# VectorE's low halves issued one step later, and one step order for both halves of the output projection

## The chip, the cores and the metric

The kernel runs on one core of a Trainium2 chip. The metric is the device time of one execution in microseconds. Before the change the median of three runs is 1422.09 us (1421.06 to 1422.41). The core has five engines that run side by side, each with its own queue in order: TensorE (PE: matrix products, and PEld, the loading of its stationary operand), VectorE (DVE), ScalarE (ACT), GpSimd (POOL) and SyncE (SP, which issues the loads here). An instruction waits on semaphores until what it needs is there, and everything behind it on its engine waits with it.

## The reference

One transformer-like encoder layer on 256 tokens of width 2048, all in float32: three attention mixers, gated and merged, an output projection with a residual, then a gated feed-forward block with a residual. What matters here:

```python
h = rms_norm(x, g_mix)
proj = h @ w_in                                   # q, k, v of three mixers, and three gates
...
mkv = rms_norm(mem, g_mem) @ w_mem_kv             # keys and values of the memory tokens
...
gates = sigmoid(gt).reshape(b, s, 3, 2048)
merged = (gates[:, :, 0] * (oa @ w_br_a) + gates[:, :, 1] * (ob @ w_br_b)
          + gates[:, :, 2] * (oc @ w_br_c))
x = x + merged @ w_o
hf = rms_norm(x, g_ffn) @ w_ffn_in                # 2 x 5632 wide
x = x + (silu(hf[..., :5632]) * hf[..., 5632:]) @ w_ffn_out
```

## The kernel before

**Precision.** TensorE takes a rounded float32 type (fp32r). Each operand is split into a high half (`whi`, ScalarE copies the value into the rounded type) and a low half (`wlo`, VectorE subtracts the high half from the value). A product is three matmuls: high by high, high by low, low by high. So every weight block of 128 x 1024 values that SP loads (tile `raw`, six buffers) needs one ScalarE copy (line 364), then one VectorE subtraction (line 365), and the high and low tiles have four buffers each, with one more in a pool of its own for every fifth block behind the merging.

**Passes.** `pair` (line 369) computes two adjoining column blocks of 512 for all 256 tokens, over a string of steps such as `STEPS_O`. Two consecutive blocks of the contraction form a pair u. A step `d` or `D` does a pair in the plain way for the first or the second column block: one load, four products, twelve matmuls. A pair can instead be done for both column blocks at once with seven products in place of eight, in the steps f, g and h and a share in p and q. These use sums of weight blocks and sums of token blocks (`forms`). On VectorE, step g begins with three adds of 128 x 512 (lines 455 to 457), step h with one (line 471), p and q with none; f, g, p and q then have one block to split and h half a block. Steps f and g issue six matmuls each, h three, p and q up to six.

The products go into six PSUM banks X, Y, Z, W, V, Q. X, Y and Z come from a pool of four banks (tag "at") and W, V and Q from another four (tag "mm"). The transposes take banks from both pools too. Behind the steps, ScalarE copies X and W out, VectorE subtracts (lines 489 and 492) and adds the banks (lines 413 and 414), and a function given by the stage takes the result.

**Order.** `run` (line 511) goes through the steps of all passes. For each step `ready()` issues the loads, the sums, the high half and the low half; the step's products are issued four steps later (three in the memory projection). The framework's planner orders each engine's instructions by its own estimates, but TensorE and SP keep program order, and `nc.follow` (line 364 on) chains the high halves on ScalarE, and the sums and low halves on VectorE, in the order of the program. Work that is not chained, such as evacuations and residual adds, the planner sets between them. Side work (transposes, squares, token sums) runs as generators that `tick` moves on by one piece behind each step's products.

**Stages.** The memory projection (`w_mem`) is a `pair` of plain steps. The projections into q, k and v and the first gates use `product`, which splits in another place (lines 125 and 126). Then `run(everything(), 4)` does the merging (four gate passes, each followed by a branch pass), the output projection in two halves (n = 0 and n = 2), and the feed-forward block: eleven passes into the hidden layer (0 to 10), with two passes of `w_ffn_out` behind passes 3, 7 and 10. Behind each w_o half VectorE adds the residual (line 785), ScalarE squares (line 791), TensorE transposes the new x block by block, and ScalarE and VectorE split the transposed block out of PSUM into `x1T` (lines 128 and 129), which the hidden passes read. Behind the first w_o half the token sums of `x1T` are formed too (lines 712 to 714 and 723).

Of the kernel before, what the change touches and what calls it, by code (L numbers as in the profile page):

```python
# [11 lines left out]
F32 = mybir.dt.float32  # L12
# [41 lines left out]
STEPS_GATE = "d0 D0 d4 D4 f1 d5 g1 D5 h1 f2 g2 d6 h2 f3 g3 h3 p0 p2 D6 q0 q2 d7 D7".split()  # L54
STEPS_FFN = "d0 D0 d1 D1 d4 D4 f2 d5 g2 D5 h2 f3 d6 g3 h3 p0 D6 q0 d7 D7".split()
STEPS_O = "d0 D0 d1 D1 f2 d4 g2 D4 h2 d5 f3 D5 g3 d6 h3 p0 D6 q0 d7 D7".split()
STEPS_O2 = "d0 f2 D0 g2 d1 h2 f3 D1 g3 d4 h3 p0 D4 q0 d5 D5 d6 D6 d7 D7".split()
STEPS_OUT = "d0 D0 d1 D1 d2 D2 f6 d3 g6 D3 h6 f7 d4 g7 h7 p0 D4 q0 d5 D5".split()
STEPS_OUT2 = "d0 f5 D0 g5 d1 h5 f6 D1 g6 d2 h6 f7 D2 g7 d3 h7 p0 p2 D3 q0 q2 d4 D4".split()

# [39 lines left out]
def encoder_block(ctx: ExitStack, tc: tile.TileContext, a: dict, out: bass.AP):  # L100
    nc = InOrder(tc)
# [10 lines left out]
    def s8(shape, name, dt=F32R, pool=None):  # L112
        return (pool or big).tile(shape, dt, name=name, tag="s8")

    def s4(shape, name, dt=F32):
        return mid.tile(shape, dt, name=name, tag="s4")
# [35 lines left out]
    def row_scale(ss, r):  # L152

        v = small.tile([P, T], F32, name="rs_v")
        nc.vector.tensor_scalar(v, ss, 1.0 / D, EPS, op0=ALU.mult, op1=ALU.add)
        y = rsqrt(v, [P, T], nc.vector)
        nc.vector.tensor_copy(r[:, 0], y)
        nc.vector.tensor_mul(r[:, 1], y, y)
# [4 lines left out]
    def advance(job):  # L163

        try:
            lag = next(job[1])
            job[0] = now[0] + (lag or 1)
            return lag is not None
        except StopIteration:
            side.remove(job)  # L170
            return True

    def start(steps):

        job = [0, steps]
        side.append(job)
        advance(job)

    def tick():
        now[0] += 1  # L180
        for job in list(side):
            if job[0] <= now[0] and advance(job):
                break

    def urgent(steps):

        while True:
            with tc.high_priority():
                try:
                    lag = next(steps)  # L190
                except StopIteration:
                    return
            yield lag
# [74 lines left out]
    def transposed(src, dst, g=None, lag=1, also=None):  # L268


        for h in range(2):
            if h:
                yield lag
            tp = bank("tp", "mm" if h and nc.on else "at")
            for k in range(2):
                for t in range(T):
                    nc.tensor.transpose(tp[:, k * S + t * P:k * S + (t + 1) * P],
                                        src[t][:, (2 * h + k) * P:(2 * h + k + 1) * P], ident)
            if g is None:
                d = dst(2 * h, 2)  # L280
                split(d[0], d[1], tp.rearrange("p (k s) -> p k s", s=S))
                if also:
                    full = s4([P, 4, P], "ffull")
                    nc.scalar.activation(full, tp.rearrange("p (b s) -> p b s", s=P), AF.Copy)
                    also(h, full)
            else:
                for k in range(2):
                    d = dst(2 * h + k, 1)
                    split(d[0], d[1], tp[:, k * S:(k + 1) * S], g(2 * h + k))
# [64 lines left out]
    def halves(*srcs):  # L354

        count[0] += 1
        pool, n = (more[0], 1) if more and count[0] % 5 == 0 else (wp, 4)
        hi = pool.tile([P, PK, NC], F32R, name="whi", bufs=n)
        lo = pool.tile([P, PK, NC], F32R, name="wlo", bufs=n)
        n = 0  # L360
        for v in srcs:
            v = v.unsqueeze(1) if len(v.shape) == 2 else v
            o = slice(n, n + v.shape[1])
            nc.follow(nc.scalar.activation(hi[:, o], v, AF.Copy))  # L364
            nc.follow(nc.vector.tensor_sub(lo[:, o], v, hi[:, o].bitcast(F32)))  # L365
            n += v.shape[1]
        return hi, lo

    def pair(src, lhs, order, done, forms=None, operand=None):

# [46 lines left out]
        def whole(u, c):  # L417
            def ready():
                if operand and c == 0:
                    operand(2 * u, True)  # L420
                raw = load((src(u, c),), 0, PK)
                if operand and c == 0:
                    if 2 * u + 2 < KT:
                        operand(2 * u + 2, True)
                    operand(2 * u)
                hi, lo = halves(raw)

                def products():
                    for k in range(2):
                        for t in range(T):  # L430
                            mul(("YV", "ZQ")[c][t], at(2 * u + k, t), hi[:, k], lo[:, k])
                return products
            return ready
# [76 lines left out]

    def run(pairs, ahead):

        nc.on = True
        waiting = []
        for p in pairs:
            for products in p:
                waiting.append(products)
                if len(waiting) > ahead:
                    waiting.pop(0)()
                    tick()  # L520
        for products in waiting:
            products()
            tick()
        nc.on = False

    whole_k = lambda n: [d + str(u) for u in range(n) for d in "dD"]
    block_pair = lambda w, n: lambda u, c: w[n + c][u]
# [146 lines left out]
    def beginning():  # L674
# [4 lines left out]
                   lambda c, r: start(take_slots(r, MEM_SLOTS[4 * c:4 * c + 4], r_m, "mem", nc.vector)), operand=memT)  # L679

    run(beginning(), 3)
    oT = [s8([P, 4, 2, S], f"oT{i}") for i in range(3)]
    ol = lambda k: (oT[k // 4][:, k % 4, 0], oT[k // 4][:, k % 4, 1])
# [33 lines left out]
    def sums_of(lhs, these, room):  # L717

        def steps():
            for u, to in zip(these, room):  # L720
                full = s4([P, 4, P], "ffull")
                for k in range(2):
                    nc.vector.tensor_add(full[:, 2 * k:2 * k + 2].rearrange("p t s -> p (t s)"),
                                         *(v.bitcast(F32) for v in lhs(2 * u + k)))
                token_sums(full, to)
                yield 1
        start(steps())
        return by_pair(these, room)
# [4 lines left out]
    def form_room(n, pool=None):  # L733
        tiles = [s8([P, 2, 2, 4, P], "forms", pool=pool) for _ in range((n + 1) // 2)]
        return [tiles[i // 2][:, i % 2] for i in range(2 * len(tiles))]
# [38 lines left out]
    def projecting():  # L774
        x.extend(s8([P, D], f"x{t}", F32) for t in range(T))
        for t in range(T):
            nc.sync.dma_start(out=x[t], in_=a["x"][t * P:(t + 1) * P, :])
        x1T.extend(s8([P, 2, 4, S], "x1T") for _ in range(4))
        mTl = lambda k: (mT[k // 4][:, 0, k % 4], mT[k // 4][:, 1, k % 4])
        oforms = sums_of(mTl, (2, 3), form_room(2))  # L780
        for n in (0, 2):
            def add(c, r, n=n):
                xc = [x[t][:, (n + c) * NC:(n + c + 1) * NC] for t in range(T)]
                for t in range(T):
                    nc.vector.tensor_add(xc[t], r[:, t], xc[t])

                def later():
                    yield 1
                    sq = s4([P, T, NC], "sq")
                    for t in range(T):  # L790
                        nc.scalar.activation(sq[:, t], xc[t], AF.Square, accum_out=ss1[:, t, n + c:n + c + 1])
                    yield 2
                    yield from transposed(xc, lambda k, m: (x1T[n + c][:, 0, k], x1T[n + c][:, 1, k]),
                                          lambda k: gT[:, 2, 4 * (n + c) + k:4 * (n + c) + k + 1], 2)
                    if n + c == 1:
                        room.extend(form_room(3))
                        forms.append(sums_of(x1l, (1, 2, 3), room[:3]))
                    elif n + c == 3:
                        yield 2
                        ssr = small.tile([P, T], F32, name="ss", bufs=1)  # L800
                        nc.vector.tensor_reduce(ssr, ss1, axis=AX.X, op=ALU.add)
                        row_scale(ssr, r_f)
                start(urgent(later()))
            yield pair(block_pair(a["w_o"], n), mTl, STEPS_O2 if n else STEPS_O, add, oforms)


    def store(t, o):
# [53 lines left out]
    def everything():  # L861
        for stage in (merging, projecting, feeding):
            yield from stage()

    run(everything(), 4)
    finish()

# [83 lines left out]
```

## Time and profile before

| what | value |
|---|---|
| median of three runs | 1422.09 us |
| the profiled execution | 1422.27 us, its span 1420.3 us |
| granted clock of TensorE, mean | 0.995 |
| TensorE busy | 1393.0 us, 98% of the span, 6248 matmuls |
| VectorE busy | 1118.9 us, 79%, 1474 instructions |
| ScalarE busy | 796.6 us, 56%, 1093 instructions |
| traffic | 277.08 MB, 195 GB/s on average |

In the profile a line names the kernel's line, the engine, the operation, the tile written and the tiles read, then the shapes. A matmul's duration overlaps with that of the next, so the distance between starts tells the pace. L75 is the line of the helper that issues all of TensorE's and SP's instructions, so TensorE's work is told apart by bank (mmX, mmY and so on) and operand. "Idle before" is time in which the engine stood still ahead of an instruction, with the instruction that ended it.

### The profile page before, as it was taken

The numbers are of one execution on the slowest core, as the hardware profiler recorded it, in microseconds if no ns is written. First come the engines' busy times: TensorE is split into PE (matmuls) and PEld (weight loads), VectorE is DVE, ScalarE is ACT, GpSimd is POOL, SyncE is SP. The second block draws the span as 40 slices with busy tenths as digits, with TensorE's granted clock in tenths as the row PEclk, the third lists the DMA queues.
The fourth block names the chain that finished last, engine by engine and source line by source line (L and its number), as shares of the span: only waits on it lengthen the run. The fifth ranks groups of instructions, "written<-read, shape, count | busy, mean of one in ns | idle before, by whom it ended". The sixth has DMA issues, their size and how long they took to land.

```text
span 1420.3 us, 17529 instructions
## 1 busy us (share of the span) xinstructions
PE 1393.0 (98%) x6248; PEld 1138.2 (80%) x6248; DVE 1118.9 (79%) x1474; ACT 796.6 (56%) x1093; POOL 76.5 (5%) x146
## 2 busy tenths in 40 slices
PE   8999999999999999997999999999999999999998
PEld 6778878888878888886888888888888888888887
DVE  6767756754788888877888888988888988988863
ACT  6756545644464564654665556554566654465642
POOL 0025532200000000000000000000000000000000
PEclk9999999999999999998999999999999999999999
DMA  8976445456565675754655557565556656555653
GB/s 297 340 237 210 152 134 174 156 168 193 183 207 178 189 229 162 281 163 133 203 178 183 192 181 236 178 194 200 189 188 207 203 184 205 193 193 195 218 174 125
DMA packets 79415, 277.08 MB, mean 195 GB/s; under 512 B 8992, under 2 KB 11552, under 8 KB 79072
## 3 DMA queue, kind: packets, MB, share of 16 engines
q1 hardware_dynamic: 79184, 275.94, 59.7%
q8 instruction: 49, 0.80, 0.2%
q14 instruction: 38, 0.31, 0.1%
q10 hardware_dynamic: 144, 0.02, 0.0%
HBM read 273.05 MB, written 2.88 MB: 194 GB/s over the span
## 4 chain that ended last, share of the span: by engine, by line
PE 79%; DVE 8%; ACT 4%; issue 4%; POOL 2%; DMA 2%; SPq 0%; ACTq 0%; DVEq 0%; POOLq 0%
PE mm L75 15%; PE mmV L75 13%; PE mmY L75 13%; PE mmZ L75 13%; PE mmQ L75 11%; PE mmX L75 8%; DVE wlo L365 3%; ACT whi L364 3%; PE mmW L75 2%; DMA raw<-in_w_mem 1%; PE tp L75 1%; DVE raw L456 1%; DVE wlo L126 1%; POOL rot L584 1%; PE sc L75 1%
## 5 line engine op out<-in xcount | busy, mean ns | idle before, releaser
L365 DVE TENSOR_TENSOR wlo<-raw,whi 128x1024 fp32r<-128x1024 f32 (+1 forms) x454 | 515.7, 1154 | 155.3 <-ACT whi L364 153.3
L364 ACT ACTIVATE whi<-raw 128x1024 fp32r<-128x1024 f32 (+1 forms) x454 | 443.1, 1000 | 339.8 <-DVE raw L471 102.1
L75 PE MATMUL mm<-whi,xT 128*128 128x512 f32 x768 | 244.1, 394 | 0.0
L126 DVE TENSOR_TENSOR wlo<-raw,whi 128x1024 fp32r<-128x1024 f32 x100 | 128.7, 1296 | 86.0 <-ACT whi L125 85.5
L75 PEld LDWEIGHTS mm<-whi,xT 128*128 128x128 f32 x768 | 144.0, 189 | 29.6 <-issue 0.8
L125 ACT ACTIVATE whi<-raw 128x1024 fp32r<-128x1024 f32 x100 | 105.6, 1070 | 89.3 <-PE mm L75 81.5
L75 PE MATMUL mm<-wlo,xT 128*128 128x512 f32 x384 | 151.0, 393 | 0.1
L75 PE MATMUL mmY<-whi,x1T 128*128 128x512 f32 x288 | 112.5, 392 | 0.0
L75 PE MATMUL mmV<-whi,x1T 128*128 128x512 f32 x288 | 109.7, 393 | 0.0
L75 PE MATMUL mmZ<-whi,x1T 128*128 128x512 f32 x224 | 87.5, 391 | 0.0
L75 PE MATMUL mmQ<-whi,x1T 128*128 128x512 f32 x224 | 87.4, 390 | 0.0
L75 PEld LDWEIGHTS mm<-wlo,xT 128*128 128x128 f32 x384 | 72.6, 189 | 15.7 <-issue 0.8
L75 PE MATMUL mmX<-whi,forms 128*128 128x512 f32 x232 | 78.9, 392 | 0.0
L365 DVE TENSOR_TENSOR wlo<-t,whi 128x1024 fp32r<-128x1024 f32 x74 | 70.7, 990 | 4.6 <-ACT whi L364 4.6
L75 PEld LDWEIGHTS mmY<-whi,x1T 128*128 128x128 f32 x288 | 54.0, 188 | 12.0
L75 PEld LDWEIGHTS mmV<-whi,x1T 128*128 128x128 f32 x288 | 54.0, 188 | 11.7
L75 PE MATMUL mmY<-whi,hT 128*128 128x512 f32 x156 | 60.6, 393 | 0.0
L364 ACT ACTIVATE whi<-t 128x1024 fp32r<-128x1024 f32 x74 | 60.6, 859 | 0.0
L75 PE MATMUL mmV<-whi,hT 128*128 128x512 f32 x156 | 60.2, 392 | 0.0
L75 PE MATMUL mmY<-wlo,x1T 128*128 128x512 f32 x144 | 56.3, 391 | 0.0
L75 PE MATMUL mmV<-wlo,x1T 128*128 128x512 f32 x144 | 56.3, 391 | 0.0
L75 PE MATMUL mmZ<-whi,hT 128*128 128x512 f32 x136 | 53.9, 396 | 0.0
(258 smaller groups left out, 2706.6 us busy)
## 6 DMA issues: line engine op xcount, KB each, us to landing
raw<-in_w_ffn SPq DMA_DIRECT2D x176, 512.0 KB, 4.1
raw<-in_w_gate SPq DMA_DIRECT2D x96, 512.0 KB, 4.2
raw<-in_w_ffn_out SPq DMA_DIRECT2D x88, 512.0 KB, 4.3
raw<-in_w_qkv SPq DMA_DIRECT2D x64, 512.0 KB, 4.5
raw<-in_w_o SPq DMA_DIRECT2D x32, 512.0 KB, 4.2
raw<-in_w_br SPq DMA_DIRECT2D x24, 512.0 KB, 3.6
raw<-in_w_mem SPq DMA_DIRECT2D x16, 512.0 KB, 6.2
rawT<-in_memT SPq DMA_DIRECT2D x8, 256.0 KB, 4.6
```

What stands on the lines that cost most here:

```text
L75: ins = op(*args, **kw)
L125: nc.scalar.activation(hi, src, AF.Copy)
L126: nc.vector.tensor_sub(lo, src, hi.bitcast(F32))
L364: nc.follow(nc.scalar.activation(hi[:, o], v, AF.Copy))
L365: nc.follow(nc.vector.tensor_sub(lo[:, o], v, hi[:, o].bitcast(F32)))
L456: nc.follow(nc.vector.tensor_add(b2[:, 0], b2[:, 0], b1[:, 0]))
L584: op(ov[:, :, :, c], ov[:, :, :, c], tmp[:, :n])
```

## The change

The low half is no longer issued together with its high half. `halves` puts it on a list, and `run` empties the list down to one entry behind each step's `ready()`; behind the last step it empties it. So each low half is issued behind the next step's sums, high half and loads. The low halves stay in their own order and in VectorE's chain. The second w_o half takes the step order of the first.

```diff
-STEPS_O2 = "d0 f2 D0 g2 d1 h2 f3 D1 g3 d4 h3 p0 D4 q0 d5 D5 d6 D6 d7 D7".split()
...
             nc.follow(nc.scalar.activation(hi[:, o], v, AF.Copy))
-            nc.follow(nc.vector.tensor_sub(lo[:, o], v, hi[:, o].bitcast(F32)))
+            due.append((lo[:, o], v, hi[:, o].bitcast(F32)))
             n += v.shape[1]
         return hi, lo
+
+    due = []
+
+    def low(n):
+
+        while len(due) > n:
+            nc.follow(nc.vector.tensor_sub(*due.pop(0)))
...
         for p in pairs:
             for products in p:
+                low(1)
                 waiting.append(products)
                 if len(waiting) > ahead:
                     waiting.pop(0)()
                     tick()
+        low(0)
         for products in waiting:
             products()
             tick()
...
-            yield pair(block_pair(a["w_o"], n), mTl, STEPS_O2 if n else STEPS_O, add, oforms)
+            yield pair(block_pair(a["w_o"], n), mTl, STEPS_O, add, oforms)
```

The order that both halves now have:

```python
STEPS_O = "d0 D0 d1 D1 f2 d4 g2 D4 h2 d5 f3 D5 g3 d6 h3 p0 D6 q0 d7 D7".split()
```

On VectorE the steps D4, g2, d5, h2 of a pass, for example, gave before: low half of D4, three adds, low half of g2, low half of d5, one add, low half of h2. They give now: three adds, low half of D4, low half of g2, one add, low half of d5, low half of h2.

## The prediction

> **What bounds the kernel now.** First the page: which engine fills the span, and the costliest VectorE group.
>
> ```profile
> span 1420.3 us, 17529 instructions
> PE 1393.0 (98%) x6248; PEld 1138.2 (80%) x6248; DVE 1118.9 (79%) x1474; ACT 796.6 (56%) x1093; POOL 76.5 (5%) x146
> L365 DVE TENSOR_TENSOR wlo<-raw,whi 128x1024 fp32r<-128x1024 f32 (+1 forms) x454 | 515.7, 1154 | 155.3 <-ACT whi L364 153.3
> ```
>
> TensorE is busy for 98% of the span, so the 153.3 us that VectorE waits for ScalarE's high halves ahead of its subtractions cannot come out of the time: only a place where TensorE itself stands still can. So next, stretches from the first matmul of one pass to that of the next (columns: stretch and length, busy time and instructions of PE, PEld, DVE, ACT, POOL, granted clock, DMA share, GB/s): the first and third gate passes, both w_o halves, then passes 0, 1, 2 and 10 into the hidden layer.
>
> ```profile
> 374.48:420.07 45.59, 43.17 (x184) 34.10 (x183) 40.49 (x54) 25.30 (x32) 0.00 (x0) 1.00 0.58 185
> 431.05:472.94 41.89, 41.89 (x184) 34.33 (x183) 37.04 (x44) 24.77 (x30) 0.00 (x0) 1.00 0.64 202
> 602.62:647.20 44.58, 44.58 (x204) 36.53 (x202) 35.92 (x43) 22.97 (x27) 0.00 (x0) 1.00 0.55 176
> 647.20:704.15 56.95, 48.72 (x203) 38.91 (x202) 43.20 (x65) 31.07 (x47) 0.00 (x0) 0.91 0.50 159
> 704.15:748.51 44.36, 44.36 (x204) 36.47 (x203) 37.95 (x62) 27.60 (x40) 0.00 (x0) 1.00 0.56 175
> 748.51:791.29 42.78, 42.78 (x193) 35.12 (x192) 37.21 (x44) 24.63 (x32) 0.00 (x0) 1.00 0.61 192
> 791.29:834.32 43.03, 42.98 (x193) 35.05 (x191) 37.75 (x45) 25.36 (x32) 0.00 (x0) 1.00 0.60 196
> 1305.99:1349.02 43.03, 42.98 (x192) 35.05 (x191) 37.76 (x44) 26.91 (x33) 0.00 (x0) 1.00 0.62 201
> ```
>
> The two w_o halves issue the same products and sixteen transposes each, yet the second is 56.95 − 44.58 = 12.4 us longer and its clock is 0.91. The first gate pass is 45.59 − 41.89 = 3.7 us longer than the third, which has the same products. Hidden passes 2 and 10 are 0.25 us longer than pass 1. These are all the places behind 374 us where TensorE stands still, except the end of the kernel. Ahead of 374 us only the memory projection uses the code that changes.
>
> **The change, part by part.**
>
> *Both w_o halves get one order.* Same steps, same loads, same instructions; only places move, so the cost is what stands still. In time order (start, length, engine, line, operation; in brackets the wait ahead and what ended it), TensorE and then VectorE in the second half (the two TensorE rows from 814 on are eleven starts apart in a hidden pass, for comparison):
>
> ```profile
> 653.65 0.55 PE L75 MATMUL tp<-ident,x 128*128 128x128 f32 x3 [1.41 <-DVE x L785]
> 657.97 0.77 PE L75 MATMUL mmZ<-whi,mT 128*128 128x512 f32 x1 [3.78 <-DVE x1T L129]
> 667.63 0.63 PE L75 MATMUL tp<-ident,x 128*128 128x128 f32 x4 [3.04 <-DVE x1T L129]
> 668.91 0.63 PE L75 MATMUL mmV<-whi,mT 128*128 128x512 f32 x1
> 669.34 0.63 PE L75 MATMUL mmV<-wlo,mT 128*128 128x512 f32 x1
> 814.33 0.39 PE L75 MATMUL mmZ<-wlo,x1T 128*128 128x512 f32 x1
> 816.82 0.40 PE L75 MATMUL mmW<-whi,forms 128*128 128x512 f32 x1
> 650.03 1.22 DVE L365 TENSOR_TENSOR wlo<-raw,whi 128x1024 fp32r<-128x1024 f32 x1
> 651.17 0.69 DVE L785 TENSOR_TENSOR x<-SB,x 128x512 f32<-128x512 f32 x1
> 651.77 1.22 DVE L365 TENSOR_TENSOR wlo<-raw,whi 128x1024 fp32r<-128x1024 f32 x1
> 652.90 0.69 DVE L785 TENSOR_TENSOR x<-SB,x 128x512 f32<-128x512 f32 x1
> ...
> 654.11 0.48 DVE L129 SCALAR_TENSOR_TENSOR x1T<-tp,gT,x1T 128x256 fp32r<-128x256 f32 x1
> 657.35 0.87 DVE L129 SCALAR_TENSOR_TENSOR x1T<-tp,gT,x1T 128x256 fp32r<-128x256 f32 x2
> ```
>
> VectorE works without a pause, but on the wrong things: the weight sums and low halves of the early seven-product steps stand between the residual adds (L785) and the evacuations (L129). The transposes wait 1.41 us for an add; bank Z, third in a pool of four behind Y and the X that the early f2 takes, waits 3.78 us for an evacuation; a later transpose waits 3.04 us. That is 8.2 us standing still; the other 4.1 of the 12.4 is mostly the clock, since matmuls then start 0.43 us apart (668.91 to 669.34) against (816.82 − 814.33) / 11 = 0.23 at full clock. With STEPS_O four whole steps come first: X is taken at step 5, the sums of g2 come at step 7, and the transposes fall behind d0, D0, d1 and D1, each with twelve matmuls to hide in. The row nearest to this is pass 0 of the hidden layer, 704.15:748.51: four whole steps, sixteen transposes, the same adds and evacuations, PE busy 44.36 of 44.36. So the 12.4 go.
>
> What may come back: the second half also carries the token sums for the hidden layer, and its VectorE work, 43.20 us, then has to fit into 44.58 us of TensorE instead of 56.95. Lower bound of a new stall: 0, if it fits (1.4 us to spare). Upper: the waits of 1.41 and 3.78 again, 5.2 us. Pass 0, with 37.95 us of work, shows none; I take 1.0. Term: −12.4 + 1.0 = −11.4. At the half's end p0 and q0 now come four and two places ahead of the last step rather than eight and six, as in the first half, which ends without a stall. SP's queue gets the same loads in another order, six raw buffers ahead of their use.
>
> *Low halves one step later.* No instruction is added. Where a step with sums follows, the previous low half waits for three adds (one ahead of an h step), and in exchange VectorE has that low half to do while ScalarE makes the next high half. VectorE in hidden pass 2, then the second matmul of g3, whose first is the one at 816.82 above:
>
> ```profile
> 798.30 0.69 DVE L365 TENSOR_TENSOR wlo<-raw,whi 128x512 fp32r<-128x512 f32 x1 [0.78 <-ACT whi L364]
> 800.30 2.36 DVE L365 TENSOR_TENSOR wlo<-raw,whi 128x1024 fp32r<-128x1024 f32 x2 [0.26 <-ACT whi L364]
> 806.43 2.36 DVE L365 TENSOR_TENSOR wlo<-raw,whi 128x1024 fp32r<-128x1024 f32 x2 [0.45 <-ACT whi L364]
> 810.17 0.69 DVE L365 TENSOR_TENSOR wlo<-raw,whi 128x512 fp32r<-128x512 f32 x1 [0.78 <-ACT whi L364]
> 811.12 2.36 DVE L365 TENSOR_TENSOR wlo<-raw,whi 128x1024 fp32r<-128x1024 f32 x2 [0.26 <-ACT whi L364]
> 813.40 0.68 DVE L455 TENSOR_TENSOR t<-raw 128x512 f32<-128x512 f32 x1
> 814.85 0.69 DVE L457 TENSOR_TENSOR t<-raw 128x512 f32<-128x512 f32 x1
> 817.27 0.50 PE L75 MATMUL mmW<-wlo,forms 128*128 128x512 f32 x1
> ```
>
> Step g3's second matmul starts 0.45 us behind its first instead of 0.23: it waits for its low half, and that makes the pass 0.25 us longer (43.03 against 42.78). Passes 2 to 10 are nine such, 9 × 0.25 = 2.3 us. The low half of D5 ends at 811.12 + 2.36 = 813.48, 0.85 ahead of the matmul that reads it (814.33 above). The three adds take 813.40 to 815.54, 2.1 us; put ahead of that low half they would make it late by 1.25. But the five waits quoted, 0.78 + 0.26 + 0.45 + 0.78 + 0.26 = 2.5 us, go away ahead of it, since a low half that is ready now stands in each. New end: 813.48 + 2.1 − 2.5 = 813.1, and g3's low half, 1.2 later, at 814.3 instead of 817.2. So TensorE waits for neither. Bounds: −2.3 (all go) to the loss of the third rival; I take −2.0.
>
> In the first gate pass the stall is at f3, g3, h3:
>
> ```profile
> 398.12 1.23 DVE L365 TENSOR_TENSOR wlo<-raw,whi 128x1024 fp32r<-128x1024 f32 x1 [0.26 <-ACT whi L364]
> 402.96 1.23 DVE L365 TENSOR_TENSOR wlo<-raw,whi 128x1024 fp32r<-128x1024 f32 x1 [1.56 <-ACT whi L364]
> 405.55 0.69 DVE L365 TENSOR_TENSOR wlo<-raw,whi 128x512 fp32r<-128x512 f32 x1 [0.76 <-ACT whi L364]
> 401.38 0.60 ACT L406 ACTIVATE SA<-mmX 128x512 f32<-128x512 f32 x1 [3.30 <-PE mmX L75]
> 402.98 0.50 PE L75 MATMUL mmW<-whi,forms 128*128 128x512 f32 x1 [0.93 <-ACT whi L364]
> ```
>
> Three of VectorE's waits there sum to 0.26 + 1.56 + 0.76 = 2.6 us, and I expect what was 3.7 to shrink to less than one. Lower bound of the gain 0.26 + 0.76 = 1.0: ScalarE's copy at 401.38 stands in its queue ahead of g3's high half and waits for TensorE; if the planner leaves it there, g3 stays late and only h3 and p0 catch up. Upper bound 3.7. I take −3.0, because the sums of g3 now run one low half (1.14 us) earlier, which gives the planner cause to put the high half first.
>
> *Elsewhere.* In the memory projection, whole steps only, a low half may go behind two splits of 128x256 (0.88 us for two at 657.35); its steps wait for loads, and no sums stand between. ±1, taken as 0. The raw buffer of a moved low half is freed up to 2.1 us later; SP's next load waits behind it, and with six buffers in flight nobody waits for that load yet.
>
> **Sum.** −11.4 − 2.0 − 3.0 = −16.4. The profiled execution took 1422.27 us (span 1420.3 and 2.0 around it), 0.2 above the median of 1422.09: 1422.27 − 16.4 = 1405.9.
>
> **Rivals.**
>
> *The stall comes back in another place*, 0.14: VectorE is overfull in the second half, or late for pass 0, and an evacuation is behind again. For it: 43.20 of 44.58 us. Against: pass 0's row. Price: 1.41 + 3.78, and 2.0 of clock (the 4.1 above was for two such), 7.2 in place of the 1.0: 1405.9 + 6.2 = 1412.1.
>
> [...]
>
> *The deferral gives nothing*, 0.14: what VectorE saves on ScalarE's round trip it loses on late whole steps, and the copy at 401.38 still holds g3. Only w_o counts: 1422.27 − 11.4 = 1410.9.
>
> *The deferral costs*, 0.06, slower: low halves behind the sums are late wherever VectorE is just in time and the round trips are not won back (the next high half then waits for something else, a copy as at 401.38). Place: the whole step or f ahead of a g.
>
> ```profile
> 1325.83 2.36 DVE L365 TENSOR_TENSOR wlo<-raw,whi 128x1024 fp32r<-128x1024 f32 x2 [0.26 <-ACT whi L364]
> 1329.03 0.39 PE L75 MATMUL mmZ<-wlo,x1T 128*128 128x512 f32 x1
> ```
>
> Read as for D5 of pass 2, 14 of the 58 have less than 2.1 us to spare; the first is f3 at 398.12, the last D5 of pass 10, above (1325.83 + 2.36 = 1328.19 against 1329.03). At 1.25 for each that is 17.5: 1422.27 − 11.4 + 17.5 = 1428.4. This decides once such a place loses more than 11.4 / 14 = 0.8 us, that is, when less than 0.45 of the 2.5 is won back. Against it: the five waits above name ScalarE's high half and nothing else.
>
> **How the numbers follow.** My forecast has 0.62, 1405.9, and by its own bounds 1403.5 to 1409. The first two rivals bring 0.28 up to 1412, the third 0.06, anything else (the planner sets a copy or an evacuation elsewhere) 0.04. All gains in full, 12.4 + 2.3 + 3.7, and 1 in the projection give 1402.9. Range: 1402.5 to 1413.5. A difference of 0.2% (2.8 us) is about what can be told from none. Faster: 0.62 + 0.28 = 0.90; slower 0.06; same 0.04.
>
> **What would show it.** The second w_o half takes about 45 us at clock 1.00, without waits of transposes for L785 or of mmZ for L129. The first gate pass takes 42 to 43 us. Passes 1 to 10 lose the wait of mmW for the low half, and VectorE's wait for L364 falls from 153.3. I am wrong if mmZ or mmQ wait for low halves ahead of a g, if w_o's second half stays above 50 us, or if pass 0 behind it grows.

## The result, and the profile after

The changed kernel takes 1403.51 us (median of four, 1403.02 to 1403.58), the kernel before beside it 1421.57 us (1420.29 to 1422.41): the ratio is 0.9873, with a 95% interval of 0.9856 to 0.9890. It is faster by 18.1 us. The forecast was 1405.9, 16.4 below the profiled execution of before, and its range of 1402.5 to 1413.5 holds the time. The profiled execution of after took 1403.52 us, its span 1401.7, so between the two profiles the span lost 18.6 us.

The page of after, with the lines that answer to those of before:

```profile
span 1401.7 us, 17524 instructions
PE 1384.8 (99%) x6248; PEld 1137.0 (81%) x6248; DVE 1118.3 (80%) x1474; ACT 807.7 (58%) x1093; POOL 76.7 (5%) x146
L373 DVE TENSOR_TENSOR wlo<-raw,whi 128x1024 fp32r<-128x1024 f32 (+1 forms) x454 | 517.9, 1154 | 106.9 <-ACT whi L363 104.6
```

The same work is there (6248 matmuls, 1474 instructions on VectorE). VectorE's wait for the high halves fell from 153.3 to 104.6 us, and most of that fall is not in the time. What is in it is seen in the stretches from first matmul to first matmul, with the columns of before: the first gate pass, the second w_o half, and passes 0, 1, 2 and 10 into the hidden layer (the pass that the prediction calls the third gate pass is the second, at 431.05 before; it and the first w_o half are unchanged, 41.89 and 44.58 us):

```profile
375.57:417.47 41.90, 41.90 (x184) 34.35 (x183) 40.33 (x54) 25.92 (x32) 0.00 (x0) 1.00 0.62 200
644.43:689.23 44.80, 44.60 (x203) 36.41 (x202) 42.15 (x65) 29.21 (x44) 0.00 (x0) 1.00 0.57 188
689.23:733.59 44.36, 44.36 (x203) 36.48 (x202) 38.37 (x63) 28.00 (x40) 0.00 (x0) 1.00 0.55 175
733.59:776.37 42.78, 42.78 (x192) 35.12 (x191) 37.17 (x45) 26.79 (x34) 0.00 (x0) 1.00 0.60 196
776.37:819.07 42.70, 42.70 (x193) 35.13 (x192) 37.68 (x45) 25.76 (x32) 0.00 (x0) 1.00 0.60 197
1287.81:1330.50 42.69, 42.69 (x192) 35.12 (x191) 37.66 (x43) 26.28 (x32) 0.00 (x0) 1.00 0.64 206
```

In every row but that of the second w_o half the first two numbers are equal: TensorE no longer stands still there. The second w_o half lost 56.95 − 44.80 = 12.15 us, and its clock is back at 1.00; the first gate pass lost 45.59 − 41.90 = 3.7; passes 2 and 10 lost 0.33 and 0.34.

*The second w_o half.* VectorE at its start, then TensorE, in order of time:

```profile
647.72 1.29 DVE L794 TENSOR_TENSOR x<-SB,x 128x512 f32<-128x512 f32 x2
648.92 0.48 DVE L128 SCALAR_TENSOR_TENSOR x1T<-tp,gT,x1T 128x256 fp32r<-128x256 f32 x1
650.46 0.48 DVE L128 SCALAR_TENSOR_TENSOR x1T<-tp,gT,x1T 128x256 fp32r<-128x256 f32 x1 [1.06 <-ACT x1T L127]
650.86 0.68 DVE L461 TENSOR_TENSOR t<-raw 128x512 f32<-128x512 f32 x1
657.08 0.48 PE L74 MATMUL mmX<-whi,mT 128*128 128x512 f32 x1
661.66 0.47 PE L74 MATMUL mmW<-whi,forms 128*128 128x512 f32 x1 [0.20 <-DVE x1T L128]
```

The residual adds (now L794) stand ahead of the first evacuations (L128), and the first weight sum (L461) behind two of them. Neither the transposes nor mmZ and mmX wait (mmX is shown, the third bank here). VectorE even idles for 1.06 us, where before it paused for only 0.15 and 0.26 us up to the evacuation at 657.35. One wait of TensorE is left, 0.20 us of mmW for an evacuation.

*A hidden pass.* VectorE and TensorE in pass 2, the stretch that answers to the one quoted before:

```profile
793.28 0.69 DVE L461 TENSOR_TENSOR t<-raw 128x512 f32<-128x512 f32 x1
795.34 2.35 DVE L373 TENSOR_TENSOR wlo<-raw,whi 128x1024 fp32r<-128x1024 f32 x2
799.41 0.39 PE L74 MATMUL mmZ<-wlo,x1T 128*128 128x512 f32 x1
801.91 0.39 PE L74 MATMUL mmW<-whi,forms 128*128 128x512 f32 x1
```

The three adds for g3 now come first (793.28 to 795.34), then the low halves of D5 and g3 in one go, with no wait for ScalarE in between. The low half of g3 ends at 795.34 + 2.35 = 797.69, and its first reader is the matmul behind 801.91, at 802.14: 4.45 us to spare, where the reader had waited. That of D5 ends one subtraction (1.14) earlier, at 796.55, 2.86 ahead of its reader at 799.41, where there were 0.85. So nothing is late in exchange: the whole chain runs earlier.

*The first gate pass.* ScalarE at the place where the copy of bank X had held it, after; then, before, the sum of g3 that its high half needs, and that high half:

```profile
401.15 1.06 ACT L363 ACTIVATE whi<-t 128x1024 fp32r<-128x1024 f32 x1
402.47 0.60 ACT L412 ACTIVATE SA<-mmX 128x512 f32<-128x512 f32 x1 [0.26 <-PE mmX L74]
```

```profile
399.98 0.69 DVE L456 TENSOR_TENSOR raw<-raw 128x512 f32<-128x512 f32 x1
401.88 1.05 ACT L364 ACTIVATE whi<-raw 128x1024 fp32r<-128x1024 f32 x1
```

The copy (now L412) waited 3.30 us for TensorE ahead of the high half of g3 before. Now the planner has put the high halves of g3, h3 and p0 first (that of p0 is shown), and the copy waits 0.26. The copy explains only a part of the old stall: the sum ended at 399.98 + 0.69 = 400.67 and the high half began at 401.88, so the copy held it for at most 1.2 us of the 3.7. No run keeps the copy in its old place under the deferral, so the split is not shown.

*Where ScalarE waits.* The view of waits (who waited for whom: us in total, times, longest us), before and then after:

```profile
ACT whi L364 <- DVE raw L471: 102.1, 48, 5.3
ACT whi L364 <- PE mmQ L75: 63.3, 48, 2.8
```

```profile
ACT whi L363 <- PE mmQ L74: 123.3, 90, 1.9
ACT whi L363 <- DVE raw L477: 48.0, 30, 4.2
```

ScalarE's wait for VectorE's add of the h steps (L471, now L477) halved, and its wait for products of TensorE doubled (for those of mmV it went from 54.6 to 113.5 us): it now stands mostly because TensorE has not yet read the buffers of the high halves and set them free, that is, because the weights are ready early.

### The profile page after: what moved, and what is told of

It is laid out like the page before. It is cut to its first block, busy times and chain, and to the rows that moved or that the text cites. A ratio compares the mean times of both kernels' runs of the same rounds, so it can differ in the third digit from the quotient of the medians.

```text
span 1401.7 us, 17524 instructions
## 1 busy us (share of the span) xinstructions
PE 1384.8 (99%) x6248; PEld 1137.0 (81%) x6248; DVE 1118.3 (80%) x1474; ACT 807.7 (58%) x1093; POOL 76.7 (5%) x146
## 4 chain that ended last, share of the span: by engine, by line
PE 92%; POOL 2%; DMA 2%; DVE 1%; ACT 1%; issue 1%; SPq 0%; DVEq 0%; ACTq 0%; POOLq 0%
PE mm L74 17%; PE mmZ L74 16%; PE mmV L74 16%; PE mmY L74 16%; PE mmQ L74 13%; PE mmX L74 9%; PE mmW L74 3%; DMA raw<-in_w_mem 2%; PE tp L74 1%; PE sc L74 1%; POOL rot L593 1%; DVE wlo L125 0%; POOL rot L590 0%; DMA rows<-in_mem 0%; PE o L74 0%
## 5 line engine op out<-in xcount | busy, mean ns | idle before, releaser
L363 ACT ACTIVATE whi<-raw 128x1024 fp32r<-128x1024 f32 (+1 forms) x454 | 451.5, 1004 | 343.2 <-PE mmQ L74 103.1
L373 DVE TENSOR_TENSOR wlo<-raw,whi 128x1024 fp32r<-128x1024 f32 (+1 forms) x454 | 517.9, 1154 | 106.9 <-ACT whi L363 104.6
```

The lines of the kernel that those rows point to most:

```text
L373: nc.follow(nc.vector.tensor_sub(*due.pop(0)))
```

## The experiments

**The theory, A.** The order of the second w_o half gives its 12 us alone, because the sums and low halves of early seven-product steps no longer stand ahead of the evacuations. The deferral gives the rest, because VectorE no longer waits out ScalarE's round trip (sum, high half, low half). The rivals: the two parts need each other; the bank that the early f2 takes does it and not the sums; the deferral works through buffers or the planner's order.

**Order only.** The kernel before, with one order for both halves.

```diff
-            yield pair(block_pair(a["w_o"], n), mTl, STEPS_O2 if n else STEPS_O, add, oforms)
+            yield pair(block_pair(a["w_o"], n), mTl, STEPS_O, add, oforms)
```

> The kernel before with STEPS_O in both w_o halves; every low half stays with its high half. Theory A (the stall in the second half is VectorE doing early sums and low halves ahead of residual adds and evacuations): the second half falls from 56.95 to 45 to 47 us, the first gate pass stays at 45.6 and the hidden passes 2 to 10 keep their 0.25 to 0.5; time 1409 to 1412. Rival B (the half is overfull for VectorE, and only the deferral makes the new order fit): the second half stays above 49 us with new waits of mmW or mmX for low halves; time 1414 or more.

Measured: 1411.60 us (1410.05 to 1412.94) against 1423.44, ratio 0.9914 (0.9896 to 0.9933). Its stretches: first gate pass, second w_o half, hidden pass 2.

```profile
376.38:422.09 45.71, 44.02 (x185) 35.29 (x183) 40.61 (x54) 25.32 (x32) 0.00 (x0) 0.96 0.57 179
649.24:693.77 44.53, 44.53 (x204) 36.53 (x202) 42.37 (x65) 28.23 (x42) 0.00 (x0) 1.00 0.57 186
780.91:823.92 43.01, 42.95 (x192) 35.05 (x191) 37.76 (x45) 25.37 (x32) 0.00 (x0) 1.00 0.59 195
```

The w_o half takes 44.53 us, all of its gain and no residual; the gate pass and the hidden pass are as before. The order needs no deferral.

**Deferral only.** The changed kernel, with before's order in the second half.

```diff
+STEPS_O2 = "d0 f2 D0 g2 d1 h2 f3 D1 g3 d4 h3 p0 D4 q0 d5 D5 d6 D6 d7 D7".split()
...
-            yield pair(block_pair(a["w_o"], n), mTl, STEPS_O, add, oforms)
+            yield pair(block_pair(a["w_o"], n), mTl, STEPS_O2 if n else STEPS_O, add, oforms)
```

> The changed kernel with STEPS_O2 back in the second w_o half. Theory A: the low halves moved do not change what stands ahead of the adds and evacuations, the second half stays at 54 to 58 us, the first gate pass falls to 42 and the hidden passes by 0.3 to 0.5 each; time 1413 to 1416. Rival B (the deferral alone clears VectorE ahead of the evacuations): second half under 50 us, time under 1409.

Measured: 1415.69 us (1415.00 to 1416.38) against 1423.44, ratio 0.9944 (0.9930 to 0.9959). The same three stretches:

```profile
375.40:417.31 41.91, 41.91 (x185) 34.34 (x183) 40.35 (x54) 25.92 (x32) 0.00 (x0) 1.00 0.62 204
644.26:701.91 57.65, 49.44 (x203) 39.31 (x202) 43.49 (x65) 30.85 (x46) 0.00 (x0) 0.91 0.51 163
789.04:831.73 42.69, 42.69 (x192) 35.13 (x191) 37.67 (x45) 25.77 (x32) 0.00 (x0) 1.00 0.60 197
```

The gate and hidden passes are those of after; the w_o half keeps its stall and is 0.7 us longer. The product of the two ratios is 0.9914 × 0.9944 = 0.9858. The last run below, which has both parts except for the deferral in the memory projection, measured 0.9858 in the same comparison: within the intervals the parts add up, and neither needs the other.

**Bank early, sums late.** The kernel before; in the second half f2 still takes bank X at the second step, but g2 and the rest come as in `STEPS_O`.

```diff
-STEPS_O2 = "d0 f2 D0 g2 d1 h2 f3 D1 g3 d4 h3 p0 D4 q0 d5 D5 d6 D6 d7 D7".split()
+STEPS_O2 = "d0 f2 D0 d1 D1 d4 g2 D4 h2 d5 f3 D5 g3 d6 h3 p0 D6 q0 d7 D7".split()
```

> The kernel before, no deferral, with the second w_o half as d0 f2 D0 d1 D1 d4 g2 and then as in STEPS_O: step f2 stays second, so X takes its bank ahead of Z, but the weight sums of g2 come seventh. Theory A (VectorE's early sums make the stall): no wait of mmZ or of the transposes above 0.5 us, second half 44.5 to 46. Rival B (the bank that X takes early makes it): mmZ still waits 2 to 4 us for an evacuation (L129), second half 48 to 53.

Measured, one execution: 1413.66 us against 1421.98. The second half, then TensorE and VectorE at its start:

```profile
647.06:695.91 48.85, 46.39 (x203) 37.67 (x202) 42.76 (x65) 29.18 (x44) 0.00 (x0) 0.97 0.54 181
```

```profile
651.62 0.62 PE L75 MATMUL tp<-ident,x 128*128 128x128 f32 x4
654.70 0.61 PE L75 MATMUL mmZ<-whi,mT 128*128 128x512 f32 x1 [2.46 <-DVE x1T L129]
651.56 1.21 DVE L365 TENSOR_TENSOR wlo<-raw,whi 128x1024 fp32r<-128x1024 f32 x1
653.09 0.68 DVE L455 TENSOR_TENSOR t<-raw 128x512 f32<-128x512 f32 x1
653.69 0.86 DVE L129 SCALAR_TENSOR_TENSOR x1T<-tp,gT,x1T 128x256 fp32r<-128x256 f32 x2
```

Bank Z, third behind X and Y, still waits 2.46 us for an evacuation that VectorE reaches only at 653.69, and half a clock follows (starts 0.43 us apart, the half's mean clock 0.97). Against the run with the order only, just the place of f2 differs, and it costs 48.85 − 44.53 = 4.3 us, so A, which expected no such wait, falls here, and B's forecast holds. This is not the bank alone: a low half (651.56) and the first sum of g2 (653.09) still stand ahead of that evacuation, and f2 issues half as many matmuls as D0, so that the second transposes come earlier (1.8 us behind the first, 651.62 − 649.80; in the changed kernel 3.2, 650.35 − 647.17).

**Sums early, bank late.** The counterpart: f2 behind the first whole pair, the sums as early as before.

```diff
-STEPS_O2 = "d0 f2 D0 g2 d1 h2 f3 D1 g3 d4 h3 p0 D4 q0 d5 D5 d6 D6 d7 D7".split()
+STEPS_O2 = "d0 D0 f2 g2 d1 h2 f3 D1 g3 d4 h3 p0 D4 q0 d5 D5 d6 D6 d7 D7".split()
```

> The kernel before, no deferral, with the second w_o half as d0 D0 f2 g2 d1 h2 f3 D1 g3 and then as in STEPS_O2: X takes its bank behind Z, but the sums of g2 still come fourth and those of g3 ninth. Theory A: the transposes still wait for the residual add (L785) or an evacuation (L129), 4 us or more in all, second half 50 to 57. Rival B: Z has its bank at once, second half 44.5 to 47.

Measured, one execution: 1421.41 us against 1421.98. The second half, then its two longest waits on TensorE, and VectorE ahead of the first:

```profile
648.76:703.23 54.47, 48.33 (x203) 38.85 (x202) 43.19 (x65) 31.06 (x47) 0.00 (x0) 0.94 0.52 163
```

```profile
659.53 0.47 PE L75 MATMUL mmX<-whi,mT 128*128 128x512 f32 x1 [3.78 <-DVE x1T L129]
666.70 0.73 PE L75 MATMUL tp<-ident,x 128*128 128x128 f32 x4 [2.11 <-DVE x1T L129]
657.76 1.23 DVE L365 TENSOR_TENSOR wlo<-raw,whi 128x1024 fp32r<-128x1024 f32 x1 [0.25 <-ACT whi L364]
658.91 0.87 DVE L129 SCALAR_TENSOR_TENSOR x1T<-tp,gT,x1T 128x256 fp32r<-128x256 f32 x2
```

Z goes free, as B said, and X, third now, waits 3.78 us, as long as Z did before: an add for an h step (at 655.07) and low halves, the last at 657.76, stand ahead of the evacuation at 658.91. The waits of the transposes themselves sum to 0.24 + 2.11 = 2.4 us, less than the 4 that A expected. The half is 54.47 − 44.53 = 9.9 us longer than with the order only, but these are not the price of the sums alone, since X is still asked for at the third step and not the fifth. Read from the kernel before, sums late take 56.95 − 48.85 = 8.1 us off and f2 behind D0 takes 56.95 − 54.47 = 2.5; the whole 12.4 needs both. So both causes are real, the sums and their low halves the larger, and they act on the same waits for evacuations. No run has the sums early and X at the fifth step, and whether the adds or their low halves weigh more was not separated.

**A longer way through ScalarE, before and after.** Two copies of 128 x 4 are chained ahead of every high half, in the kernel before and in the changed one.

```diff
+    pad = const.tile([P, 2, 4], F32, name="pad")
+    nc.vector.memset(pad, 0.0)
...
+            for _ in range(2):
+                nc.follow(nc.scalar.activation(pad[:, 1], pad[:, 0], AF.Copy))
             nc.follow(nc.scalar.activation(hi[:, o], v, AF.Copy))
```

> The kernel before with two ScalarE copies of 128x4 chained ahead of each high half, about 0.2 us each, so that a high half comes about 0.4 us later; the extra copies feed nothing. Theory A (what the deferral wins in the gate and hidden passes is ScalarE's round trip): five waits ahead of g3 grow by 0.4, so each hidden pass from 2 to 10 is 1.5 to 2 us longer; time 1435 to 1455. Rival B: ScalarE is 56% busy and hides it, time within 5 us of before.

> The changed kernel with the same two extra copies. Theory A: a deferred low half of 1.14 us stands where VectorE waited, so most of the added 0.4 us is covered; 1404 to 1409, that is, at least 15 us less growth than in the kernel before. Rival B (the gain has another source): it grows as much as the kernel before with the same copies.

Measured: before with the copies 1444.48 us (1443.54 to 1446.45) against 1421.98, ratio 1.0158 (1.0140 to 1.0175); after with them 1403.15 us (1401.43 to 1405.79), against 1403.51 without and a little under the 1404 to 1409 that A expected. The view of waits of the kernel before, then of before with the copies, and ScalarE in the latter:

```profile
PEld mmW L75 <- DVE wlo L365: 5.7, 10, 1.1
```

```profile
PEld mmW L75 <- DVE wlo L369: 18.2, 21, 1.1
```

```profile
800.20 1.04 ACT L368 ACTIVATE whi<-raw 128x1024 fp32r<-128x1024 f32 x1
801.49 1.05 ACT L368 ACTIVATE whi<-raw 128x1024 fp32r<-128x1024 f32 x1
```

Two high halves in a row now start 1.29 us apart (801.49 − 800.20). The copies need no data, so where a high half waits for a sum they run in that wait and cost nothing there: the two ahead of the high half at 805.62, 0.42 us together, start at 802.44, and it still waits 1.57 us for its sum. The edit delays chiefly the high halves behind another. Before, these started about 1.0 apart (two take 2.00), so the delay is 0.3 us each and not the 0.4 expected. Even so the loads of low halves for bank W, which the g steps use, wait 18.2 us in place of 5.7, those for X, which p and q use too, 14.9 in place of 1.8, and the kernel loses 22.5 us. By stretches, hidden passes 2 to 10 lose 13.2 us (0.98 to 2.34 each, against the 1.5 to 2 expected), the four passes of `w_ffn_out`, which the change itself does not shorten, 8.6, and pass 1 1.4; the second w_o half is 3.9 us shorter (53.06), for a reason that stays open. With the deferral the same copies cost nothing that can be measured in the time (its first gate pass is 0.7 us longer, 42.56). That is the mechanism of the prediction, shown: before, ScalarE's time was part of the chain that feeds the steps g, p and q; with a low half to do meanwhile it no longer is, up to this delay.

**Two steps of deferral.**

```diff
-                low(1)
+                low(2)
```

> The changed kernel with each low half issued two steps behind its high half instead of one. Theory A (one step already covers ScalarE's round trip; more only makes low halves later): 1403 to 1405, and the smallest distance of a whole step's low half ahead of its matmul in the hidden passes falls from 2.4 to about 1. Rival B (each further step of delay costs TensorE at every g): 1408 or more.

In the first gate pass f3, g3 and h3 are adjacent, so there the low half of f3's second block is formed behind the add of h3 into that block: the instructions are the same, but the values differ, so this variant no longer computes the layer and serves only for its time.

Measured: 1408.89 us (1407.14 to 1410.06), ratio 0.9896 (0.9880 to 0.9911), 5.8 above the run beside it with one step (1403.13, below; in the memory projection it has none). The number is the rival's, the mechanism is not: by the starts and ends of its rows every low half of the w_o halves and of hidden passes 1 to 3 is ready 2.6 us or more ahead of its reader. Stretches of the second w_o half and of hidden pass 2, then TensorE and VectorE in pass 2:

```profile
643.83:689.87 46.04, 44.76 (x203) 36.45 (x202) 42.25 (x65) 29.39 (x44) 0.00 (x0) 1.00 0.56 180
777.01:820.38 43.37, 42.85 (x192) 35.04 (x191) 37.58 (x45) 26.08 (x31) 0.00 (x0) 1.00 0.61 194
```

```profile
784.48 0.63 PE L74 MATMUL tp<-ident,SA 128*128 128x128 f32 x4 [0.52 <-DVE SA L841]
782.51 0.69 DVE L461 TENSOR_TENSOR t<-raw 128x512 f32<-128x512 f32 x1
783.11 1.22 DVE L841 TENSOR_TENSOR SA<-SA,SB 128x1024 f32<-128x1024 f32 x1
```

The gate product (L841), which is not chained, now stands behind the next step's first add, and the transposes of it wait 0.52 us. That makes pass 2 0.67 us longer, and it is so in seven passes (2, 3, 5, 6, 7, 9, 10), 0.66 to 0.76 us in each and 4.9 in all; with 46.04 − 44.80 = 1.24 in w_o, where an evacuation is late in the same way, that is 6.1 us and accounts for the whole difference. Here one step is enough to cover ScalarE; a second only moves the other work of VectorE.

**The projection as before.** The changed kernel, with the low halves of the memory projection issued at once.

```diff
-    def run(pairs, ahead):
+    def run(pairs, ahead, late=1):
...
-                low(1)
+                low(late)
...
-    run(beginning(), 3)
+    run(beginning(), 3, 0)
```

> The changed kernel, but in the memory projection each low half is issued with its step again. There the profile of the changed kernel shows the sixteen steps ending 1.2 us later than before. Theory A (the deferral holds low halves behind operand splits): the projection ends at 53.2 instead of 54.4 and the time falls by about 1.1, to 1402.4. Rival B (the loads land when they land; one execution differs from the next): no change, 1403.5, and the projection's end scatters with the landing of the mem rows.

Measured: 1403.13 us (1402.82 to 1404.53), ratio 0.9858 (0.9843 to 0.9873): no difference from the changed kernel, as B said. The last product of the projection ends at 54.27 us here, 54.55 in the changed kernel, 53.38 before and 55.43 with the order only. The 1.1 us by which its first gate pass begins later (375.57 against 374.48) is not the deferral's, since this kernel begins it at 375.13 and the one with the order only, which defers nothing, at 376.38.

## Why the prediction was right, and where it was off

- **The w_o order**, −11.4: it was −12.15. The step was right: the waits of the transposes and of the bank go, and the half clock with them (mean 0.91 before, 1.00 after). Of the residual, put at 1.0 between 0 and 5.2, 44.80 − 44.58 = 0.22 came, all but 0.02 of it mmW's wait. Both causes that it names are shown to matter: with f2 left early, late sums take 8.1 us off, and with the sums late, f2 at the fifth step takes another 4.3. They are not shown one without the other, since weight work stands in the wait of the first run and an early third bank in that of the second. One reading was too strong: VectorE was not quite "without a pause" (0.15 and 0.26 us).
- **The hidden passes**, −2.0, with −2.3 as the bound: they gave −3.6. The mechanism was right and the term mis-sized, in the step "passes 2 to 10 are nine such, 9 × 0.25". Pass 1 is not the floor: passes 2 and 10 now take 42.70 and 42.69, below its 42.78. And only 2 and 10 had been read, so the sentence that named all the places where TensorE stands still was wrong: pass 4 had lost more. Its stretch before, and after:

```profile
963.06:1005.47 42.41, 42.18 (x184) 34.25 (x183) 38.08 (x46) 23.63 (x29) 0.00 (x0) 1.00 0.61 201
```

```profile
947.43:989.31 41.88, 41.88 (x184) 34.32 (x183) 37.96 (x47) 24.35 (x29) 0.00 (x0) 1.00 0.63 201
```

  It gained 0.53, pass 8 0.52 and pass 9 0.48. The working by waits was too cautious as well: counted from the start of pass 2, g3's low half ended 1.7 us earlier than the forecast's 814.3 (797.69 − 776.37 = 21.32 against 814.3 − 791.29 = 23.0). Two more waits of VectorE lie among the five that were counted, 0.36 us at 799.36 and 0.70 at 803.96, both for ScalarE's half of a transposed block, and they went too; where the other 0.6 us come from stays open.
- **The first gate pass**, −3.0: it was −3.7, the upper bound. The planner did put the high half of g3 ahead of the copy, though the copy had held it for 1.2 us at most. The fourth gate pass, not in the sum, gave another 0.2 (43.91 to 43.73).
- **The memory projection**, 0 ± 1: +1.1 in the profile. Issuing its low half at once again changes nothing, so it is scatter of the start, not a cost of the change.
- **The sum**: −12.15 − 3.6 − 3.7 − 0.2 + 1.1 = −18.5 against −18.6 in the spans. The 2.2 us beyond the forecast are 1.6 of hidden passes, 0.75 of w_o and 0.9 of gates, less 1.1 of projection. All three gains came out larger than forecast, and that the total is off by no more is in part luck, since the later start of one profile took 1.1 back.
- **The rivals.** The stall does not come back: 44.80 at clock 1.00. The deferral gives something: 7.8 us alone by the medians, and 5.9 between the spans, where its first gate pass begins 0.9 later. It costs nothing: with one step the tightest low half of pass 2 has 2.36 us. The nearest thing to the third rival is the second step of deferral, and there it is the gate product, not a low half, that is late.
- **What was to show it.** W_o at about 45 us, the gate pass at 42 to 43 (41.90, just under), mmW's wait for its low half gone, VectorE's wait below 153.3: all seen. From the first gate pass on, the view of waits of after lists no wait of TensorE for a low half.

## What to carry to other kernels

Where one engine makes a sum, a second converts it and the first must finish the job, put an independent piece of the first engine's work between its two turns. Here the chain A, B, A without it paid B's time where the consumer had no slack, and a delay added to B showed it: two copies ahead of each high half cost 22.5 us before the change and nothing that can be measured after it. In this kernel one such piece was enough: with two, the work that nobody chained (here the gate product) came late, and the time rose by 5.8 us. Where a stage begins with evacuations and residual adds, give it plain steps first, so that the evacuations do not stand behind weight sums while a third bank is waiting for them: here that took the second w_o half from 56.95 to 44.53 us. And read the floor of a pass from every pass of its kind, not from its neighbour.

## What the runs showed of the hardware that was not expected

*The clock falls after short gaps, and not each time.* TensorE in the first gate pass of the kernel with the order only:

```profile
403.56 0.40 PE L75 MATMUL mmY<-whi,xT 128*128 128x512 f32 x1
404.88 0.50 PE L75 MATMUL mmW<-whi,forms 128*128 128x512 f32 x1 [0.93 <-ACT whi L364]
406.14 0.54 PE L75 MATMUL mmW<-wlo,forms 128*128 128x512 f32 x1 [0.76 <-DVE wlo L365]
406.90 0.63 PE L75 MATMUL mmZ<-whi,forms 128*128 128x512 f32 x1
409.89 0.40 PE L75 MATMUL mmX<-wlo,forms 128*128 128x512 f32 x1
```

Two waits of 0.93 and 0.76 us with one matmul between them were followed by starts 0.43 apart until about 409.9; the pass's clock is 0.96. In the kernel before the same waits at the same place left it at 1.00, and so did the 1.28 us that mmW waits in w_o with two steps of deferral. The pass is hardly longer for it (45.71 against 45.59): the slower matmuls run in time in which TensorE would have waited, 45.59 − 43.17 = 2.4 us of waits before and 45.71 − 44.02 = 1.7 here. With bank early and sums late, as above, no product starts for 3.3 us (651.39 to 654.70, with the transposes at 651.62 between), the wait in it is 2.46, and half a clock follows.

The half clock lasts some 3.4 us (406.5 to 409.9), and none of the gaps ahead of it is longer than 1.4 us from one start to the next (403.56 to 404.88, 404.88 to 406.14). The four transposes at 651.62 did not keep the clock up, which is no test of transposes, since shorter gaps without them brought half a clock as well. What decides whether a gap brings it is not shown.

*The first stage scatters.* The first gate pass begins at 374.48, 375.57, 376.38 and 375.40 us in four of the profiles above, in no order that follows the change: differences of a microsecond in a span cannot be put down to an edit here without a look at that start.
